# The stores of v, of the output gates and of the merge gates issued by ScalarE in place of SP

## The chip, the core and the metric

The kernel runs on one core of one Trainium2 chip. A core has five engines that take their instructions each in its own order: TensorE (PE), VectorE (DVE), ScalarE (ACT), GpSimd (POOL) and SyncE (SP), and 16 DMA engines that move data between on-chip memory and device memory. A transfer is begun ("issued") by one of the engines' queues; in the kernel before, all of them are issued by SP. The metric is the device time of one execution in microseconds (us), lower is better.

## What is computed

One layer of an encoder with 2048 tokens of width 1024, in fp32. Three token mixers run on one normalised input; their projections are merged by gates, and a squared-ReLU MLP follows. Cut to what matters here:

```python
h = rmsnorm(x, g_mix)
z = h @ w_in
qk_m, v_m, o_m, i_pre, f_pre, qkv_na, q_mem, gate_pre = jnp.split(z, split_idx, axis=-1)
...
h_m = rmsnorm(h_fwd + h_bwd, g_mlstm.reshape(MLSTM_HEADS, MLSTM_V_DIM))
h_m = (h_m.reshape(bsz, s, MLSTM_V_W) * jax.nn.sigmoid(o_m.astype(jnp.float32))).astype(x.dtype)
...
gates = jax.nn.sigmoid(gate_pre).reshape(bsz, s, N_BRANCH, D_MODEL)
y = (gates[:, :, 0] * (h_m @ w_proj_mlstm)
     + gates[:, :, 1] * (h_na @ w_proj_na)
     + gates[:, :, 2] * (h_mem @ w_proj_mem))
x = x + y @ w_out

u = rmsnorm(x, g_ffn) @ w_up
return x + jnp.square(jax.nn.relu(u)) @ w_down
```

`h_fwd` and `h_bwd` are the two directions of an mLSTM over chunks of tokens, which uses `v_m`; `h_na` is attention over a neighbourhood of the token grid with a table of biases, `h_mem` attention to 256 memory tokens.

## The kernel before

**Arithmetic.** A product of fp32 matrices is made of three passes (`mm3`, L233 to L235): each operand is split into a rounded part and a remainder, by ScalarE (a copy) and VectorE (a subtraction). Weights come in units of 512 KB: `fetch` loads a raw unit `wr` (L173, three buffers), ScalarE and VectorE make the split weights `ws` of it (L177, L178, five buffers), and `take` hands them out some units ahead of their use.

**Phases.** Phase 1 goes over four blocks of 512 tokens (`block_a`): query and key for the neighbourhood attention, the convolved query and key of the mLSTM, their value parts, `v`, in blocks 2 and 3 the 24 merge gates, then the output gates. Beside these matmuls, at each `tick`, run pieces of side work: attention units over the grid (their loads `naq`, `nak`, `nav`, and the bias tables `nab`; matmuls at L1055, L1074, L1088), memory attention, and the preparation of the next block (`prep_x` loads `xt`, L463; VectorE normalises it, L418; L435 and L436 split it into `hT`). Between the merge gates of blocks 2 and 3, `sums_down` makes sums of the weights for the MLP: it loads two `xt` tiles (two buffers, L463), VectorE combines them (L583), and they are stored to `s_t`. Phase 2 is the mLSTM by chunks of 128 tokens in both directions (`ml_chunk`, with its loads `qk`, `v`, `rb`, `wb`; the exponentials of decay `de` at L821), its row work by blocks (`ml_rows`: loads `r_f` and `r_i`, scans on VectorE at L754 and L760, `r_b` at L764 stored to `s_r`, `r_w` at L773 stored to `s_w`), and beside them the merge gates of blocks 1 and 0 (`late_gates`). Phase 3 merges, projects, and runs the MLP; `load_mix` loads the branch outputs (L1283) and `merge` loads the gates again (L1294).

**The tiles in question.** A product of `v`, of an output gate or of a merge gate stands in a PSUM bank of tag `mm` (two banks in phases 1 and 2). ScalarE writes it into a tile `ev` of 128 x 512 floats, 256 KB (two buffers in phases 1 and 2), by a copy (L538) or a tanh (L561, L603), and it is stored to device memory: 16 stores of `v` (`s_v`), 16 of output gates (`s_o`) and 96 of merge gates (`s_g`). All go through the helper `store` (L103), as do many other stores of the kernel.

**Order.** Only PE's order is written by hand. The instructions of the other engines, and the DMAs that an engine issues, are ordered by a scheduler which goes by priorities (`cur_priority`) and by its own estimate of when operands are there. An engine takes its list strictly in order. Each transfer is given one of eight semaphores in turn, whichever engine issues it, and is not issued before the earlier transfer on the same semaphore has landed.

Of the kernel before, what the change touches and what calls it, by code (L numbers as in the profile page):

```python
# [34 lines left out]
NAB = 4  # L35
LATER_3 = 4
STORE = 'sync'
ORDER_0 = (2, 3, 0, 1)
WSP, WRAW, AHEAD = 5, 3, 5
NB = S // TB  # L40
# [42 lines left out]
class Body:  # L83
# [15 lines left out]
    def ev(self):  # L99
        return self.t("ev", [128, 512], self.ev_bufs)  # L100

    def store(self, dst, src):
        getattr(self.nc, STORE).dma_start(dst, src)  # L103

    def ps(self, tag, shape=(128, 512)):
        self.n += 1
# [266 lines left out]
    def phase_1(self):  # L373
# [3 lines left out]
        nc.scalar.activation(p_a.tile([128, 16], F32, name="warm"), self.mhalf, AF.Exp)  # L377
        self.xorder = [(0, t) for t in ORDER_0] + [(b, t) for b in range(1, NB) for t in range(4)]
        self.xhs = []
# [110 lines left out]
    def block_a(self, b):  # L490


        nc, a = self.nc, self.a
        hT = self.hT
        w = self.take(4)
        for i, t in enumerate(ORDER_0 if b == 0 else range(4)):
            if i == 0 or b == 0 and i < 3:
                self.trans_x()
            if b == 0 and i == MEM_R:
                self.mem_rms()  # L500
            p = self.tok_group(hT, w, t)
            z = self.t("zna", [128, 512], 4)
            nc.scalar.activation(z, p, AF.Copy)
            self.qkq.append(self.na_qk(b, t, z.rearrange("p (a b) -> p a b", b=32)))
        if b + 1 < NB:
            rms = self.rms_x(b + 1)
            self.jobs += [lambda: next(rms, None), None] * 10
        if b in SPILL:
            for k in range(8):
                self.jobs += [lambda k=k: self.store(self.scr["hT"][b][:, :, k], hT[:, :, k].bitcast(F32)), None]  # L510
        for c in range(4):
            self.conv(b, c, self.ch_group(self.take(1)[0], hT))
        w = self.take(4)
        zif = self.t("zif", [128, 4, 16], 1)
        for t in range(4):
            p = self.tok_group(hT, w, t, slice(0, 256), 4)
            s = self.ev()[:, 0:256]
            nc.scalar.activation(s, p, AF.Copy)

            for half in range(2):  # L520
                for r in range(2):
                    p0 = r * 64 + half * 24
                    self.store(self.scr["vna"][half, 8 * b + 2 * t + r], s[p0:p0 + 40])
            p = self.tok_group(hT, w, t, slice(256, 528), 4)
            z = self.t("zm", [128, 256], 4)
            nc.vector.tensor_copy(z, p[:, 0:256])
            nc.scalar.activation(zif[:, t], p[:, 256:272], AF.Copy)  # L527
            self.memq.append(self.mem_unit(b, t, z))
        for g in {0: [0], 1: [1, 2], 2: [3, 4], 3: [5, 6, 7]}[b]:
            self.na_ready.append(g)  # L530
        self.jobs += [None, None, lambda: self.if_rows(b, zif)]
        w, sums = self.take(4), None
        for t in range(4):
            if t == PREP_V and b + 1 < NB and b not in GATES_1:
                self.prep_x()
            p = self.tok_group(hT, w, t)
            s = self.ev()
            nc.scalar.activation(s, p, AF.Copy)  # L538
            self.store(self.scr["v"][b][t * 128:(t + 1) * 128], s)
            if b == NB - 1 and t % 2 == 0:  # L540
                sums = sums or self.sums_down(15)
                sums = next(sums, None) and sums
        if b in GATES_1:
            sums, qs = None, list(range(7)) if b + 1 < NB else list(range(7, 15))
            for j in range(24):
                if j == 22 and b + 1 < NB:
                    self.prep_x()
                self.gate(b, j)
                if j < 21 or b + 1 == NB:
                    if j % 3 != 1:  # L550
                        sums = sums or self.sums_down(qs.pop(0))
                        sums = next(sums, None) and sums
        w = self.take(4)
        for t in range(4):
            if t:
                self.trans_x()
            if t < 3:
                self.prep_x()
            p = self.tok_group(hT, w, t)
            s = self.ev()  # L560
            nc.scalar.activation(s, p, AF.Tanh, scale=0.5)  # L561
            self.store(self.scr["og"][b][t * 128:(t + 1) * 128], s)
            if b == NB - 1:
                ts = slice(t * 128, (t + 1) * 128)
                src = self.scr["hT"][GATES_2[0]]
                if t < 3:
                    nc.sync.dma_start(hT[:, :, :, ts].bitcast(F32), src[:, :, :, ts])
                else:
                    for k in range(0, 8, 2):
                        for l in range(2):  # L570
                            nc.sync.dma_start(hT[:, l, k:k + 2, ts].bitcast(F32), src[:, l, k:k + 2, ts])
# [27 lines left out]
    def gate(self, b, j, w=None, hT=None, cuts=(0, TB)):  # L599

        p = self.ch_group(w or self.take(1)[0], hT or self.hT, cuts)
        s = self.ev()
        self.nc.scalar.activation(s, p, AF.Tanh, scale=0.5)  # L603
        self.store(self.scr["gate"][b][j], s)

    def late_gates(self, more):

# [982 lines left out]
```

## Time and profile before

| | |
|---|---|
| Time, median of 3 runs | 2939.38 us (2939.16 to 2945.97) |
| The profiled execution: its time | 2945.09 us |
| Its span | 2943.4 us |
| PE busy | 2895.3 us (98%) |
| DVE busy | 2005.5 us (68%) |
| ACT busy | 1186.6 us (40%) |
| POOL busy | 210.0 us (7%) |
| Moved by DMA | 632.00 MB, 215 GB/s |

The page gives busy times of the engines over the span. A view of waits lists, for each engine, what ended its idle time ("waited for"), and for SP how long its next DMA stood in the queue before it could be issued. A timeline lists instructions with their start, and in brackets the idle time before them. PEclk is the clock that was granted to TensorE as a share of its full 2.4 GHz.

### The profile page before, as it was taken

The numbers are of one execution on the slowest core, as the hardware profiler recorded it, in microseconds if no ns is written. First come the engines' busy times: TensorE is split into PE (matmuls) and PEld (weight loads), VectorE is DVE, ScalarE is ACT, GpSimd is POOL, SyncE is SP. The second block draws the span as 40 slices with busy tenths as digits, with TensorE's granted clock in tenths as the row PEclk, the third lists the DMA queues.
The fourth block names the chain that finished last, engine by engine and source line by source line (L and its number), as shares of the span: only waits on it lengthen the run. The fifth ranks groups of instructions, "written<-read, shape, count | busy, mean of one in ns | idle before, by whom it ended". The sixth has DMA issues, their size and how long they took to land.

```text
span 2943.4 us, 41858 instructions
## 1 busy us (share of the span) xinstructions
PE 2895.3 (98%) x15052; PEld 2370.3 (81%) x15052; DVE 2005.5 (68%) x3471; ACT 1186.6 (40%) x2256; POOL 210.0 (7%) x382
## 2 busy tenths in 40 slices
PE   8999999999989999999999999999999999999999
PEld 7888888778868777778888888888788888888887
DVE  6676865477754545655688888666686988886666
ACT  6465654355543333432243333533312433344332
POOL 4121210021000112310000000000000000000000
PEclk9999999999999999999999999999999999999999
DMA  8786778867899777878444445766864444466654
GB/s 287 215 278 201 243 234 249 266 210 221 264 286 300 260 236 233 259 227 303 140 135 157 158 158 194 250 192 221 290 208 117 147 151 154 156 228 219 191 189 161
DMA packets 344976, 632.00 MB, mean 215 GB/s; under 512 B 29664, under 2 KB 151456, under 8 KB 344768
## 3 DMA queue, kind: packets, MB, share of 16 engines
q1 hardware_dynamic: 344768, 629.32, 66.7%
q8 instruction: 119, 1.95, 0.3%
q14 instruction: 89, 0.73, 0.1%
HBM read 452.58 MB, written 176.62 MB: 214 GB/s over the span
## 4 chain that ended last, share of the span: by engine, by line
PE 53%; DVE 1%; DMA 1%; issue 1%; ACT 0%; SPq 0%; POOL 0%; DVEq 0%; ACTq 0%
PE mm L233 18%; PE mm L234 18%; PE mm L235 18%; PE mm L1353 0%; DMA ev<-in_x_dram 0%; DMA wr<-in_w_units_dram 0%; DVE ev L1509 0%; DVE acc L1502 0%; DMA X<-s_a 0%; DVE ws L178 0%; DVE ev L1364 0%; DVE ev L1365 0%; DVE X L1359 0%; DVE ev L1331 0%; PE pn L872 0%
## 5 line engine op out<-in xcount | busy, mean ns | idle before, releaser
L233 PE MATMUL mm<-X,ws 128*128 128x512 f32 x896 | 348.9, 389 | 0.0
L235 PE MATMUL mm<-X,ws 128*128 128x512 f32 x896 | 348.6, 389 | 0.0
L234 PE MATMUL mm<-X,ws 128*128 128x512 f32 x896 | 348.6, 389 | 0.0
L178 DVE TENSOR_TENSOR ws<-wr,ws 128x1024 fp32r<-128x1024 f32 (+1 forms) x194 | 239.1, 1240 | 132.8 <-ACT ws L177 131.4
L233 PE MATMUL mm<-hT,ws 128*128 128x512 f32 (+1 forms) x712 | 293.8, 413 | 0.7 <-ACT ev L561 0.7
L234 PE MATMUL mm<-hT,ws 128*128 128x512 f32 (+1 forms) x712 | 278.4, 391 | 0.3 <-DMA hT<-s_hT 0.3
L235 PE MATMUL mm<-hT,ws 128*128 128x512 f32 (+1 forms) x712 | 278.6, 391 | 0.0
L233 PE MATMUL mm<-ws,hT 128*128 128x512 f32 (+2 forms) x704 | 259.2, 368 | 3.5 <-ACT zif L527 2.1
L177 ACT ACTIVATE ws<-wr 128x1024 fp32r<-128x1024 f32 (+1 forms) x194 | 204.2, 1057 | 121.7 <-PE mm L235 81.9
L235 PE MATMUL mm<-ws,hT 128*128 128x512 f32 (+2 forms) x704 | 249.1, 354 | 2.0 <-DVE hT L436 2.0
L234 PE MATMUL mm<-ws,hT 128*128 128x512 f32 (+2 forms) x704 | 248.3, 353 | 0.0
L235 PE MATMUL mm<-X 128*128 128x512 f32 x600 | 233.5, 389 | 0.5 <-DVE X L1476 0.5
L233 PE MATMUL mm<-X 128*128 128x512 f32 x600 | 233.5, 389 | 0.1
L234 PE MATMUL mm<-X 128*128 128x512 f32 x600 | 233.4, 389 | 0.0
L203 ACT ACTIVATE ws<-wr 128x512 fp32r<-128x512 f32 x224 | 135.0, 628 | 219.9 <-PE mm L235 139.8
L1475 ACT ACTIVATE X<-X 128x1024 fp32r<-128x1024 f32 x108 | 114.7, 1062 | 207.5 <-DMA X<-s_t 66.4
L233 PEld LDWEIGHTS mm<-X,ws 128*128 128x128 f32 x896 | 168.2, 188 | 35.1
L235 PEld LDWEIGHTS mm<-X,ws 128*128 128x128 f32 x896 | 168.2, 188 | 34.9
L234 PEld LDWEIGHTS mm<-X,ws 128*128 128x128 f32 x896 | 168.2, 188 | 34.6
L1476 DVE TENSOR_TENSOR X<-X 128x1024 fp32r<-128x1024 f32 x108 | 131.6, 1223 | 80.1 <-ACT X L1475 79.5
L1502 DVE TENSOR_TENSOR acc<-acc,mm 128x512 f32<-128x512 f32 x192 | 126.3, 684 | 68.7 <-PE mm L235 68.6
L235 PEld LDWEIGHTS mm<-hT,ws 128*128 128x128 f32 x712 | 134.2, 188 | 29.9
(286 smaller groups left out, 6028.6 us busy)
## 6 DMA issues: line engine op xcount, KB each, us to landing
wr<-in_w_units_dram SPq DMA_DIRECT2D x290, 512.0 KB
s_s<-u SPq DMA_DIRECT2D x32, 1024.0 KB
s_g<-ev SPq DMA_DIRECT2D x96, 256.0 KB
ev<-s_g SPq DMA_DIRECT2D x96, 256.0 KB
s_a<-u SPq DMA_DIRECT2D x96, 256.0 KB
X<-s_s SPq DMA_DIRECT2D x42, 512.0 KB
nab<-in_rpb_dram SPq DMA_DIRECT2D x96, 220.0 KB
X<-s_a SPq DMA_DIRECT2D x33, 512.0 KB
```

Source lines behind the costliest of these rows:

```text
L177: nc.scalar.activation(w[:, 0], raw, AF.Copy)
L178: nc.vector.tensor_tensor(w[:, 1], raw, w[:, 0].bitcast(F32), ALU.subtract)
L203: nc.scalar.activation(hi, src, AF.Copy)
L233: mm(out, lhs[0], rhs[0], start=first, stop=False)
L234: mm(out, lhs[0], rhs[1], start=False, stop=False)
L235: mm(out, lhs[1], rhs[0], start=False, stop=last)
L1475: nc.scalar.activation(hi, src, AF.Copy)
L1476: nc.vector.tensor_tensor(lo, src, hi.bitcast(F32), ALU.subtract)
L1502: nc.vector.tensor_tensor(c, c, p, ALU.add)
```

## The change

`store` takes the queue as an argument, and the three calls that store `v`, the output gates and the merge gates name ScalarE. All other stores and all loads stay with SP.

```diff
 STORE = 'sync'
+OWN = 'scalar'
...
-    def store(self, dst, src):
-        getattr(self.nc, STORE).dma_start(dst, src)
+    def store(self, dst, src, queue=STORE):
+        getattr(self.nc, queue).dma_start(dst, src)
...
             nc.scalar.activation(s, p, AF.Copy)
-            self.store(self.scr["v"][b][t * 128:(t + 1) * 128], s)
+            self.store(self.scr["v"][b][t * 128:(t + 1) * 128], s, OWN)
...
             nc.scalar.activation(s, p, AF.Tanh, scale=0.5)
-            self.store(self.scr["og"][b][t * 128:(t + 1) * 128], s)
+            self.store(self.scr["og"][b][t * 128:(t + 1) * 128], s, OWN)
...
         self.nc.scalar.activation(s, p, AF.Tanh, scale=0.5)
-        self.store(self.scr["gate"][b][j], s)
+        self.store(self.scr["gate"][b][j], s, OWN)
```

A new line 38 moves all later lines down by one (L103 becomes L104). PE's order stays the same. 128 DMAs leave SP's list for ScalarE's, and the scheduler, which plans anew, also moves other instructions of SP, ScalarE, VectorE and GpSimd. Three places of it follow; the numbers at the end of names tell tiles apart.

SP at the end of block 2, before: the last output gates of the block are stored (`s_o`), the loads of bias tables (`nab`) and of the next block's tokens (`xt`) come between raw weights (`wr`).

```order
L463 DMA xt_6794<-in_xT_dram 128x1024
L173 DMA wr_6731<-in_w_units_dram 128x1024
L1046 DMA nab_0_0_2_6820<-in_rpb_dram 128x440
L103 DMA s_o_90<-ev_6853 128x512
L1046 DMA nab_0_0_3_6882<-in_rpb_dram 128x440
L103 DMA s_o_90<-ev_6915 128x512
L1038 DMA nav_0_1_6927<-s_vna 120x3x128
L1039 DMA nav_0_1_6927<-s_vna 80x128
L1046 DMA nab_0_1_0_6937<-in_rpb_dram 128x440
L103 DMA s_o_90<-ev_6990 128x512
L173 DMA wr_6993<-in_w_units_dram 128x1024
L463 DMA xt_6856<-in_xT_dram 128x1024
```

And SP at the same place after the change:

```order
L464 DMA xt_6794<-in_xT_dram 128x1024
L1022 DMA naq_1_7123<-s_qs 32x4x256
L1047 DMA nab_0_0_3_6882<-in_rpb_dram 128x440
L464 DMA xt_6856<-in_xT_dram 128x1024
L1023 DMA nak_1_7124<-s_ks 32x4x704
L1022 DMA naq_1_7123<-s_qs 32x4x256
L1047 DMA nab_0_1_0_6937<-in_rpb_dram 128x440
L174 DMA wr_6731<-in_w_units_dram 128x1024
```

The stores are gone from the list, the load `xt_6856` stands three places behind `xt_6794` instead of eleven, and `wr_6731`, which stood ahead of it, comes behind it.

ScalarE in phase 2, before: between two merge gates (`ev`, L603) stand the exponentials of decay (`de`, L821), the denominators (`sm`) and copies (`sk`) of the chunks.

```order
L603 ACTIVATE ev_11759<-mm_11669 128x512
L821 ACTIVATE de_2114_11883<-rb_2086_11754,r_a_2012_11433 128x128 x2
L892 ACTIVATE sm_11804<-pn_11774 128x2
L821 ACTIVATE de_2114_11883<-rb_2086_11754,r_a_2012_11433 128x128
L892 ACTIVATE sm_11804<-pn_11775 128x2
L821 ACTIVATE de_2114_11883<-rb_2086_11754,r_a_2012_11433 128x128
L841 ACTIVATE sk_2062_11655<-mx_11821 128x2x128
L841 ACTIVATE sk_2062_11655<-mx_11822 128x2x128
L603 ACTIVATE ev_11857<-mm_11767 128x512
```

After the change:

```order
L604 ACTIVATE ev_11759<-mm_11669 128x512
L774 ACTIVATE r_w<-r_w 36x512
L104 DMA s_g_92<-ev_11759 128x512
L822 ACTIVATE de_2114_11883<-rb_2086_11754,r_a_2012_11433 128x128
L893 ACTIVATE sm_11804<-pn_11774 128x2
L893 ACTIVATE sm_11804<-pn_11775 128x2
L822 ACTIVATE de_2114_11883<-rb_2086_11754,r_a_2012_11433 128x128 x3
L842 ACTIVATE sk_2062_11655<-mx_11821 128x2x128
L842 ACTIVATE sk_2062_11655<-mx_11822 128x2x128
L604 ACTIVATE ev_11857<-mm_11767 128x512
L851 ACTIVATE sk_2062_11655<-mx_11837 128x256
L104 DMA s_g_93<-ev_11857 128x512
```

Behind each gate now stands its store, one or two places later, and the exponential of the third row unit (`r_w`), which before stood some 20 rows further on, stands between the first of these gates and its store.

SP at the same time, before: the store of the second of these gates, then the loads of the third row unit (`r_f`, `r_i`), whose result goes to `s_r_146` 15 rows below the end of this piece.

```order
L103 DMA s_g_93<-ev_11857 128x512
L750 DMA r_f<-s_lf 4x512
L750 DMA r_i<-s_ig 4x512
L103 DMA s_hf_102<-h_2119_11903 128x512
L809 DMA v_2128_11942<-s_v_85 128x4x128
L750 DMA r_f<-s_lf 4x512
L750 DMA r_i<-s_ig 4x512
```

After the change these loads stand some rows above the piece that follows, which begins with the `r_f` loads of the fourth row unit:

```order
L751 DMA r_f<-s_lf 4x512 x2
L807 DMA qk_2127_11940<-s_qk 128x4x128
L104 DMA s_r_146<-r_b 4x4x128
L104 DMA s_sk_118<-sk_2040_11557 128x768
L174 DMA wr_12156<-in_w_units_dram 128x1024
L813 DMA rb_2172_12145<-s_r_145 128x512
L104 DMA s_hf_112<-h_2098_11810 128x512
L810 DMA v_2107_11849<-s_v_86 128x4x128
```

The row units have moved up against the chunks: the result `s_r_146` now stands ahead of the stores `s_sk_118` and `s_hf_112` and of the load `v_2107`, which all stood ahead of it before.

## Rows read from the trace of the kernel before

**Rows 1.** Busy time, share and instructions of each engine (the page, part 1).

```profile
PE 2895.3 (98%) x15052; PEld 2370.3 (81%) x15052; DVE 2005.5 (68%) x3471; ACT 1186.6 (40%) x2256; POOL 210.0 (7%) x382
```

**Rows 2.** Phases 1 to 3: us, busy PE, PEld, DVE, ACT, POOL; PEclk, DMA share, GB/s.

```profile
0.00:957.00 957.00, 927.54 (x5867) 766.67 (x5868) 612.58 (x1366) 489.48 (x1021) 138.16 (x260) 0.99 0.80 250
957.00:1349.00 392.00, 385.04 (x2156) 296.25 (x2155) 209.25 (x465) 147.42 (x472) 71.88 (x122) 0.99 0.79 249
1349.00:2944.00 1595.00, 1582.70 (x7033) 1307.42 (x7031) 1183.64 (x1640) 549.70 (x764) 0.00 (x0) 1.00 0.56 185
```

**Rows 3.** Waits of PE, whole span: us in total, times, longest.

```profile
PE mx L1055 <- DMA s_g<-ev: 8.5, 1, 8.5
...
PE mm L235 <- DVE hT L436: 2.0, 1, 2.0
...
PE mm L233 <- ACT ev L561: 0.7, 1, 0.7
PE mm L233 <- ACT ev L603: 0.7, 1, 0.7
...
PE mm L233 <- ACT ev L538: 0.4, 1, 0.4
```

**Rows 4.** SP's issues from 870 us: start, us, count.

```profile
870.73 1.59 SPq L463 DMA_DIRECT2D xt<-in_w_units_dram  x2
...
874.47 0.64 SPq L1022 DMA_DIRECT2D nak<-s_ks  x1
...
879.41 0.34 SPq L103 DMA_DIRECT2D s_g<-ev  x1
```

**Rows 5.** Waits of SP's queue, whole span: us in total, times, longest.

```profile
SPq L103 <- ACT ev L603: 85.7, 37, 4.8
...
SPq L463 <- DMA s_t<-xt: 33.2, 20, 4.2
...
SPq L103 <- ACT ev L538: 29.9, 12, 5.2
...
SPq L103 <- ACT ev L561: 21.6, 11, 3.1
```

**Rows 6.** Groups of ScalarE by form: busy us, mean ns, idle us before.

```profile
L603 ACT ACTIVATE ev<-mm 128x512 f32<-128x512 f32 x96 | 56.8, 591 | 115.3 <-issue 58.1 <-PE mm L235 51.2 <-DMA s_g<-ev 5.3
```

**Rows 7.** SP's issues in phase 2, two merge gates in a row.

```profile
1005.19 0.59 SPq L103 DMA_DIRECT2D s_g<-ev  x1
...
1014.06 0.54 SPq L103 DMA_DIRECT2D s_g<-ev  x1
```

**Rows 8.** SP's issues at the end of block 2.

```profile
605.20 0.33 SPq L173 DMA_DIRECT2D wr<-in_w_units_dram  x1
...
614.01 0.33 SPq L463 DMA_DIRECT2D xt<-in_xT_dram  x1
```

**Rows 9.** VectorE's timeline at 618 us, the wait in brackets.

```profile
618.91 2.98 DVE L418 SCALAR_TENSOR_TENSOR xt<-xt,gmix,gbc 128x128 f32<-128x128 f32 x8 [0.84 <-DMA xt<-in_xT_dram]
```

**Rows 10.** Engines busy in three stretches around 618 us.

```profile
614.00:618.00 4.00, 2.81 (x12) 1.69 (x10) 3.63 (x10) 2.13 (x5) 0.84 (x2) 1.00 0.77 252
618.00:623.90 5.90, 3.59 (x17) 2.76 (x17) 5.06 (x15) 2.52 (x6) 3.56 (x4) 1.00 0.79 286
623.90:627.00 3.10, 2.88 (x9) 2.50 (x10) 1.88 (x7) 1.24 (x3) 0.13 (x1) 0.53 0.84 210
```

**Rows 11.** Engines busy in two stretches around 883 us.

```profile
874.30:883.00 8.70, 0.29 (x2) 0.00 (x0) 2.68 (x4) 0.00 (x0) 0.00 (x0) 0.63 1.01 230
883.00:885.60 2.60, 2.48 (x6) 2.08 (x7) 0.84 (x4) 0.66 (x2) 0.00 (x0) 0.50 1.05 406
```

**Rows 12.** SP's issues at the end of phase 2.

```profile
1341.31 1.63 SPq L1283 DMA_DIRECT2D X<-s_hmem  x2
```

**Rows 13.** SP's issues for the third row unit.

```profile
1060.56 0.46 SPq L750 DMA_DIRECT2D r_f<-s_lf  x1
...
1081.34 0.78 SPq L103 DMA_DIRECT2D s_r<-r_b  x2
```

## The prediction

> **What bounds the kernel now.** I read the page's busy shares first. PE is busy 2895.3 us of the 2943.4 us span, ScalarE only 1186.6 us [rows 1]. PE runs the same matmuls in the same order in both kernels, so the change can only move the 48.1 us in which PE stands, and the time that the clock gate takes. Then I cut the span in three stages [rows 2]. PE idles 29.5 us in phase 1 (957.00 less 927.54), 7.0 us in phase 2 (392.00 less 385.04), 12.3 us in phase 3. Phase 3 issues none of the moved stores. So the reachable idle time is at most 36.5 us.
>
> The waits of PE say what ended its idle time [rows 3]. Waits for `ev` tiles (their eviction, and behind it a free buffer) sum to 0.7 + 0.7 + 0.4 = 1.8 us. The largest wait, 8.5 us, is put down to a gate store, but L1055 does not read that tile. It reads `nak` and `naq`; their last load was issued at 874.47, the store only at 879.41 [rows 4]. The store's semaphore event was merely the last one seen. So the stores are not what PE waits for. What they do hold is SP: it stood for a gate, v or output gate tile 85.7 + 29.9 + 21.6 = 137.2 us [rows 5]. Loads queued behind those stores on SP start late, and that is the only way in which the old place of the stores can reach PE.
>
> **The change part by part.** All 128 stores leave SP. One issue holds SP 0.34 us (the store at 879.41 [rows 4]) to 0.59 us (at 1005.19 in phase 2 [rows 7]), so 128 x 0.34 = 44 us of issuing go at the least, 76 us at the most, with up to 137.2 us of standing. None of this is PE time in itself.
>
> *ScalarE gets 128 issues.* The trace before has no DMA issue on ScalarE; the nearest row is SP's issue of the same store. By it ScalarE carries 44 to 76 us more, at most 1263 us of 2943. An issue sits behind an eviction of 591 ns [rows 6], and the next ScalarE instruction starts that much later, also where PE waits for it; but gate stores follow each other at 8.9 us (1005.19 to 1014.06 [rows 7]), and the `mm` tag has two PSUM banks, so an issue is covered: taken as 0. If the cover were gone, all 128 in PE's way would cost 44 to 76 us; nothing in the 1.8 us of waits suggests that. The store now also waits for ScalarE's own write, and for the place of an earlier transfer: see the slower rival.
>
> *The stall at 614 to 627.* SP took the load of raw weights `wr` at 605.20 and the token load `xt` only at 614.01 [rows 8]. VectorE's normalisation of that tile (L418) waited for the load until 618.91 [rows 9], then L436 made `hT`, for which PE waited 2.0 us [rows 3]. Across the three stretches [rows 10] PE idled 4.00 - 2.81, 5.90 - 3.59 and 3.10 - 2.88, in all 3.7 us, and ran the last 3.10 us at a granted 0.53 (near the 1.2 GHz level, after the standing), which loses 1.5 us: 5.2 us together. In the changed order this `xt` load stands ahead of that weight load, with no output gate store before it. I take the whole 5 us off (bounds 0 and 5.2). Late next is the weight load, which moves behind a few loads of 0.3 to 0.4 us each.
>
> *The stall at 874 to 883.* It costs 8.70 - 0.29 us idle, and 2.60 us at a granted 0.50 after it, 1.3 us: 9.7 us [rows 11]. What was late was two `xt` loads at 870.73, waiting for the store of the sums before them (L463 behind `s_t`: 33.2 us in 20 waits [rows 5]); the `nak` loads queue behind [rows 4]. The changed order keeps `xt` ahead of `nak`, and no moved store lies between them. Taken: 0; bounds -9.7 (if sums are made earlier, so that the sums' store lands earlier) and +2.
>
> *Phase 2.* SP's queue interleaves a gate store with the loads of each chunk and the row units. Without the stores these loads come forward by several places. PE idles 7.0 us here at a mean granted clock of 0.99 [rows 2], which is some 4 us more: 11 us can be gained at most, the rest is in rival 2. I take -3, because no wait of PE in this stage is put down to a DMA.
>
> *The merge.* The loads that phase 3 starts on go out up to 1341.31 [rows 12], beside the last gate stores. A store issued at once from ScalarE takes a share of the DMA engines just there. Bounds 0 and +6 (near the 8.7 us that the `nak` loads took under a full DMA share of 1.01 [rows 11]); taken +3. The Trainium skill, "DMA: Bandwidth & Descriptors", section "Queues, rings and completion order", says that each DMA engine takes turns between the rows it has work for, and SP and ScalarE have a row each; by that the store would even overtake loads that SP issued first. The page of the profile shows one hardware queue, so no run here shows it.
>
> The sum is -5 + 0 - 3 + 3 = -5 us against the profiled execution of 2945.1 us, so 2940. That execution lies 5.7 us above the median of 2939.4; against the median the forecast is 2934.4, rounded to **2935**.
>
> **The rivals.** *1. Faster: SP really was the brake.* If sums (VectorE) and loads in blocks 2 and 3 all come forward, the 874 stall goes too: -9.7 with -5, and half of phase 2's 11, -5: about -20, 2919. For it: SP stood 137.2 us for these tiles [rows 5]. Against: VectorE, not SP, often sets when a raw buffer is free, and the `s_t` landing stays.
>
> *2. Slower: ScalarE stands in order for a transfer of SP.* Every DMA takes one of eight semaphores in turn, so a store waits until the transfer eight places before it has landed. Before, both were in one queue; now ScalarE stands if SP has not yet got there, and behind it stand the decay exponentials (L821), the copies and the evictions. The place is the row unit of phase 2: before, its load `r_f` went at 1060.56 and the store of its result `s_r` at 1081.34 [rows 13], 20.8 us of VectorE work apart, with weight, `rb` and `v` loads issued between. In the changed order the next row unit's `r_f` loads and this `s_r` store stand early, ahead of such loads, so SP may stand for VectorE, VectorE for the landing of `s_r`, and ScalarE for the weight load behind. It decides from a wait of about one gate's period, 8.9 us [rows 7]: of a wait of some 16 us, 7 would reach PE. Two such row units are left at that point, so 14 us, and about 2 us of lower clock after each, as at 883 [rows 11]: +18. With the -5 at 614 that is +13, 2952. For it: the orders. Against: the row loads come forward with the store, and then `r_b` is ready when SP comes to it.
>
> *3. No effect.* The loads are early enough anyway, and the stall at 614 only changes its releaser: within 3 us of 2939. The Trainium skill, same page, section "Issuing engines are not separate DMA queues", says that starting DMAs from several engines saves only the issuing sequencer's time; by it the change is worth SP's time of issuing, of which PE pays nothing, so 2939. The rows agree as far as PE's 1.8 us of `ev` waits go; they differ in that SP's standing came to at least 1.8 times its issuing (137.2 against 76).
>
> **How the numbers follow.** A difference of 0.3% (8.8 us) is about what a measurement of this kernel can tell from none. Chances: my forecast (some -10 to +5 us) 0.31, rival 3 0.12; both lie within 0.3%, giving 0.43. Rival 1 and mixtures beyond -8.8 us: 0.30. Rival 2: 0.27. The range goes from rival 1's 2919 to a little beyond rival 2's 2952, as its waits could be longer: 2956. Cut off are all stalls gone at once (-27 us) and a ScalarE that stands at many stores. The likeliest case's own range is 2929 to 2944.
>
> **What would show it.** Right: PE idle at 614 to 627 nearly gone and no granted clock of 0.53 there; the stall near 874 to 883 still there; SP's waits for `ev` gone; ScalarE with idle time in front of its next instruction after a store, but no PE wait for `ev` above 3 us. Rival 1 shows as PE idle in phase 1 under 20 us. Rival 2 shows as PE idle in phase 2 well above 7.0 us, with waits for ScalarE's or VectorE's tiles (L821, L841, `ev`) between 1045 and 1130. The forecast is wrong if the total moves by over 9 us, or if the 614 stall stays and something else pays.

## The result, and the profile after

The changed kernel takes 2950.07 us, the kernel before beside it on the same chip 2942.52 us (medians of 20 runs each): a ratio of 1.0024, 95% interval 1.0015 to 1.0033. It is slower by 7.6 us, where the forecast had -5. The time lies inside the range on record, the change has the other sign. The profiled execution took 2956.77 us with a span of 2954.9 us, 11.5 us above the span before. It lies 6.7 us above its kernel's median, the traced execution of the kernel before 2.6 us above that kernel's, so losses read by comparing the two traces are some 4 us too large in sum.

The page after, parts 1, 3 and 6, first. PE, VectorE and ScalarE do the same work as before [rows 1], and a second hardware queue, q10, has taken 33.56 MB, the 128 stores of 256 KB.

```profile
PE 2896.2 (98%) x15052; PEld 2369.9 (80%) x15052; DVE 2009.1 (68%) x3471; ACT 1187.7 (40%) x2256; POOL 207.0 (7%) x382
...
q1 hardware_dynamic: 326336, 595.75, 63.3%
q10 hardware_dynamic: 18432, 33.56, 3.2%
...
s_g<-ev ACTq DMA_DIRECT2D x96, 256.0 KB
```

The same three stages as in [rows 2] (us, then the busy time of PE, PEld, DVE, ACT, POOL, then PEclk, DMA share, GB/s), after:

```profile
0.00:957.00 957.00, 930.52 (x5886) 769.84 (x5887) 612.07 (x1370) 492.70 (x1026) 138.38 (x260) 0.99 0.81 252
957.00:1349.00 392.00, 371.40 (x2098) 283.10 (x2097) 211.13 (x460) 143.43 (x464) 68.57 (x122) 1.00 0.76 235
1349.00:2955.00 1606.00, 1594.25 (x7071) 1316.94 (x7069) 1185.89 (x1641) 551.54 (x767) 0.00 (x0) 1.00 0.56 186
```

PE idles 26.5, 20.6 and 11.8 us in them, before 29.5, 7.0 and 12.3. So phase 1 gained 3.0 us, phase 2 lost 13.6, phase 3 is as it was. The granted clock is the same, near 2.4 GHz in all three.

**Phase 1** went as forecast. Two windows after, around the two stalls of [rows 10] and [rows 11]; then PE's timeline at the second one (the wait in brackets):

```profile
614.00:627.00 13.00, 11.72 (x59) 9.43 (x58) 9.38 (x25) 7.86 (x18) 6.42 (x7) 1.00 0.88 271
874.00:886.00 12.00, 7.07 (x27) 5.80 (x28) 5.05 (x13) 3.58 (x8) 0.13 (x1) 0.72 0.92 262
```

```profile
878.93 0.61 PE L1056 MATMUL mx<-nak,naq 96*128 96x320 f32 x1 [7.71 <-DMA nab<-in_rpb_dram]
```

At 614 to 627 PE's idle time fell from 3.7 to 1.3 us, and the granted clock of 0.53 is gone. The idle time went with the change: over the same matmuls (from 610 to 635 us in the kernel before) PE stands 0.2 to 1.3 us in the four kernels of this document that store from ScalarE in phase 1 in the new order, and 2.6 to 3.8 us in the eleven others. The low clock is less certain: the clock granted from 608 to 632 us is 0.93 in the kernel before and in "phase 2 alone" below, but 1.00 in the swapped kernel below, and both of these leave phase 1 as it was. Nor do the 3.0 us of the whole phase stand clear by themselves, since the ten kernels that leave phase 1 as it was idle 25.8 to 31.2 us there. At 874 PE still stands 7.71 us for loads of the attention unit, now put down to one of them (`nab`) and not to a gate store.

**Phase 2** is where the time went. The waits of PE between 957 and 1349 us (total, times, longest), first of the kernel before, then after:

```profile
PE tr L914 <- DVE hm L917: 2.6, 3, 2.2
...
PE mx L848 <- ACT sk L841: 0.7, 1, 0.7
```

Of the changed kernel, the waits of PE over the whole span, where the lines are one higher; the `hm` and the L849 waits are all in phase 2:

```profile
PE tr L915 <- DVE hm L918: 10.0, 7, 2.6
...
PE mx L849 <- ACT sk L842: 4.3, 2, 3.2
...
PE mm L234 <- DVE hm L918: 2.0, 1, 2.0
```

10.0 - 2.6, 4.3 - 0.7 and 2.0 make 13.0 of the 13.6 us. `hm` is the end of a chunk: PE transposes its four heads into a bank `tr`, ScalarE (L917) and VectorE (L918) split it into the one buffer `hm`, which two transfers store to `s_hm`; then the next chunk's transposes may follow. The view of this tile, 1150 to 1345 us, before and after (first and last start of each operation; then what its engines stood for, and who stood for it):

```profile
L916 ACT ACTIVATE hm<-tr x16: 572/578/600, 1189.5 to 1319.1; 128x512 fp32r<-128x512 f32 x16
...
its engine sat idle before it (us, times) until:
  ACT hm L916: 4.2, 1
  DMA s_hm<-hm: 0.6, 1
```

```profile
L917 ACT ACTIVATE hm<-tr x16: 571/578/601, 1189.0 to 1330.8; 128x512 fp32r<-128x512 f32 x16
...
  DMA s_hm<-hm: 9.1, 4
  ACT hm L917: 5.7, 2
who waited for it (us, times):
  PEld tr L915: 13.5, 9
  PE tr L915: 10.0, 7
```

The first of the sixteen starts at the same time in both (1189.5, 1189.0), the last 11.7 us later. Followed back over this stretch, the chain that ended last does not run over PE after; two transfers, `s_hm` (14.6% of it) and `og` (11.7%), are its largest named parts (start, us, what):

```profile
1213.33 5.05 DMA s_hm<-hm
...
1222.31 2.99 DMA og<-s_o
1225.40 1.03 DVE og L864
...
1234.93 5.82 DMA s_hm<-hm
...
1252.15 4.07 DMA og<-s_o
```

The longest single wait of PE in phase 2 comes earlier, at a row unit. Its `r_b` scans now stand ahead of `pt` (L840) in VectorE's list, and `pt` and `sk`, which read a chunk's scores, free the PSUM banks of PE's next transposes (L849). VectorE and then PE, after:

```profile
991.46 1.26 DVE L755 TENSOR_TENSOR_SCAN r_b<-reset,r_f 4x512 f32<-4x512 f32 x1 [9.96 <-DMA r_f<-s_lf]
992.65 0.72 DVE L840 TENSOR_TENSOR pt<-mx,de 128x256 f32<-128x256 f32 x2
```

```profile
993.51 0.44 PE L849 MATMUL mx<-ident,qk 128*128 128x128 f32 x2 [3.18 <-ACT sk L842]
```

VectorE stood 9.96 us for the unit's load and PE 3.18 us behind it. In the kernel before the same `pt` runs at 992.52, the scans of this unit only from 999.77, and PE has no such wait.

So PE waits for tiles of VectorE and ScalarE, and these wait for stores and loads of the chunks and of the row units. The prediction had looked only at the first half of that sentence. Two causes can lie behind it: SP's list and VectorE's list are *ordered* differently without the stores (by the two traces some 100 rows of SP and 75 of VectorE from 957 us on have another place), or the large stores now stand in a *second queue* beside SP's loads and other stores. A third is the issue itself, on ScalarE.

### The profile page after: what moved, and what is told of

Its sections match the earlier page's. It is cut to its first block, busy times and chain, and to the rows that moved or that the text cites. A ratio compares the mean times of both kernels' runs of the same rounds, so it can differ in the third digit from the quotient of the medians.

```text
span 2954.9 us, 41863 instructions
## 1 busy us (share of the span) xinstructions
PE 2896.2 (98%) x15052; PEld 2369.9 (80%) x15052; DVE 2009.1 (68%) x3471; ACT 1187.7 (40%) x2256; POOL 207.0 (7%) x382
## 3 DMA queue, kind: packets, MB, share of 16 engines
q10 hardware_dynamic: 18432, 33.56, 3.2%
## 4 chain that ended last, share of the span: by engine, by line
PE 82%; DMA 7%; DVE 5%; issue 2%; ACT 1%; POOL 1%; SPq 0%; POOLq 0%; DVEq 0%; ACTq 0%
PE mm L234 25%; PE mm L236 25%; PE mm L235 25%; PE tr L1075 2%; DMA wr<-in_w_units_dram 1%; DMA s_hm<-hm 1%; DMA s_t<-xt 1%; PE mx L1089 1%; PE mx L1056 1%; DMA qk<-s_qk 1%; DVE ws L179 1%; PE pn L873 1%; DMA xt<-in_w_units_dram 1%; POOL rs L328 1%; PE mx L1226 1%
```

## The experiments

Ratios are to the kernel before on the same chip, with their 95% intervals; the text says "idle" for PE's idle time in the stage 957 to 1349 (392.00 less busy PE), 7.0 us before and 20.6 us after. Diffs are against the changed kernel unless said otherwise.

**Phase 1 alone, phase 2 alone.** The 80 stores of phase 1 from ScalarE and the late gates from SP, and the reverse.

```diff
-    def gate(self, b, j, w=None, hT=None, cuts=(0, TB)):
+    def gate(self, b, j, w=None, hT=None, cuts=(0, TB), queue=OWN):
...
-        self.store(self.scr["gate"][b][j], s, OWN)
+        self.store(self.scr["gate"][b][j], s, queue)
...
-            self.gate(GATES_2[i], j, self.gw, self.h2[i], cuts)
+            self.gate(GATES_2[i], j, self.gw, self.h2[i], cuts, STORE)
```

> Only the 80 stores of phase 1 (v, output gates, merge gates of blocks 2 and 3) go by ScalarE; the 48 late gates stay with SP. In the profiles the changed kernel was 4.5 us ahead of the old one at the start of phase 2 and lost 13 us from there to 1331 us. Theory A (the loss is made in phase 2): this kernel keeps the lead, 2 to 6 us below the kernel before (ratio 0.998 to 0.9995), PE idle in phase 2 near 7 us. Rival B (any move of this kind shakes the whole plan, the place of the loss is chance): the phase 2 part is not near 7 us, ratio anywhere within 0.3%.

> Only the 48 late gates of phase 2 go by ScalarE, phase 1 is as before. Theory A: slower by 8 to 14 us (ratio 1.003 to 1.005), PE idle in phase 2 about 20 us, waits of the transposes (L915) for hm near 10 us. Rival B: no such sum; within 3 us of the kernel before.

Measured: phase 1 alone 0.9990 (0.9979 to 1.0001), phase 2 alone 1.0060 (1.0044 to 1.0075). The stage 957 to 1349 of the two:

```profile
957.00:1349.00 392.00, 384.31 (x2157) 295.02 (x2156) 209.86 (x461) 143.24 (x466) 71.50 (x122) 0.99 0.80 249
```

```profile
957.00:1349.00 392.00, 374.46 (x2110) 286.36 (x2109) 210.92 (x464) 147.56 (x470) 70.00 (x122) 0.99 0.76 234
```

Idle 7.7 and 17.5 us. The loss comes with the 48 late gate stores (15.7 us by the medians). Those of phase 1 are worth a little (3.6 us by the medians, an interval that just reaches 1). The two add up to +12.1 us where the change itself has +7.6, a difference that the intervals allow.

**The same large stores in the old order.** The scheduler's order is held by giving SP something to issue where the store was: one 2 KB row of the same tile (a "token", to a scratch tensor that nobody reads). Against the kernel "phase 2 alone":

```diff
+            tok=[d(f"s_tok{j}", [1, 512]) for j in range(24)],
...
+        if b in GATES_2:
+            self.store(self.scr["tok"][j], s[0:1])
```

> As phase 2 only, but SP also stores one row (2 KB) of each late gate's tile to a spare place. With this SP waits for the tile and issues a DMA just where it did before, and the planner gives all engines the order of the kernel before; the 256 KB still go by ScalarE. Theory O (the loss comes from the new order of SP and VectorE): within 3 us of the kernel before, PE idle in phase 2 near 7 us. Theory Q (it comes from the second queue, ScalarE's 0.33 us per issue or its waits for a place): as slow as phase 2 only, +8 to +14 us.

Measured: 1.0019 (1.0006 to 1.0032), idle 11.0 us: between the two. With tokens beside all 128 stores:

> All 128 stores by ScalarE as in the change, with a 2 KB token by SP beside each one, so that nearly the whole old order stays. Theory O: within 4 us of the kernel before, neither the gain at 614 us nor the loss in phase 2. Theory Q: +5 to +12 us.

Measured: 1.0043 (1.0027 to 1.0058). PE's idle time in phase 1 is 33.6 us here (957.00 less 923.44), 4 above before: in the old order the second queue brings no gain in phase 1 (over the matmuls of the first stall PE stands 3.4 us), so the gain there goes with the new order. This loss was not taken apart further.

**ScalarE's issues.** The kernel before with one more ScalarE operation behind each late gate, 0.31 us in the trace, the price of an issue (0.327 us at the median in the changed kernel):

```diff
+        if b in GATES_2:
+            junk = self.p_a.tile([128, 128], F32, name=f"junk{b}_{j}", tag="junk", bufs=1)
+            self.nc.scalar.activation(junk, self.ident, AF.Copy)
```

> The kernel before, with a copy of 128 x 128 floats (about 0.31 us) on ScalarE behind each of the 48 late gates, into a spare tile; stores stay with SP and the order of all engines stays (two rows differ). It measures ScalarE's time for an issue (0.33 us) by itself. If the 4.8 us that the token kernel of phase 2 lost are ScalarE's time: +3 to +6 us (ratio 1.001 to 1.002). If they come from the second queue or the waits for a place: within 2 us.

Measured: 1.0004 (0.9991 to 1.0017). No cost of ScalarE's time shows. The interval still reaches 5 us; the swapped kernel below, with 48 real issues on ScalarE (of 0.20 us, a smaller transfer), leaves room for some 2 us.

**Which half of phase 2.** The token for some of the late gates only, so that the new order begins late (the condition below), or ends early (`<= 20` in place of `> 20`):

```diff
+        if b in GATES_2 and len(self.gq) > 20:
+            self.store(self.scr["tok"][j], s[0:1])
```

> Late gates by ScalarE, with SP's token beside the first 27 of the 48, so that the old order stays up to about 1190 us and the new order comes after. Theory H (the loop of h, hm and og in the second half of phase 2 is what the new order hurts): some +10 us, most of what phase 2 only lost beyond the token kernel; PE's waits for hm near 8 us. Rival F (the row units at the start of phase 2): as the token kernel, +4 to +6 us.

> The other way round: the token beside the last 21 late gates, so that the new order stands up to about 1190 us and the old one after. Theory H: +4 to +7 us. Rival F: +10 us or more, made before 1010 us. If both halves matter alike: each of the two kernels near +10 us.

Measured: new order in the second half 1.0014 (1.0005 to 1.0023), in the first half 1.0034 (1.0021 to 1.0047); idle 13.0 and 15.4 us. The theory that the loop with the single `hm` buffer at the end of the phase carries the loss (H) fell: the new order in the second half alone adds nothing to the token kernel's 1.0019. That the first half costs more is not shown so clearly, as its interval meets those of the other half and of the token kernel. Nor is the time lost only where the order is new: of the 8.4 us of idle time that the kernel with the new order in the first half has above before, 4.8 lie behind 1200 us.

**Two buffers for `hm`.** If PE only waits because the next chunk's `hm` waits for the store of the last, a second buffer for its rounded part should give most back.

```diff
-        hm = self.t("hm", [128, 2, 4, 128], 1, F32R)
-        nc.scalar.activation(hm[:, 0], p, AF.Copy)
-        nc.vector.tensor_tensor(hm[:, 1], p, hm[:, 0].bitcast(F32), ALU.subtract)
+        hm = [self.t("hm%d" % l, [128, 4, 128], 2 - l, F32R) for l in range(2)]
+        nc.scalar.activation(hm[0], p, AF.Copy)
+        nc.vector.tensor_tensor(hm[1], p, hm[0].bitcast(F32), ALU.subtract)
...
```

> The change, with the first half of the tile hm (written by ScalarE at L917) in two buffers instead of one, so that ScalarE no longer waits for the landing of the store of the tile before. If the landing of these stores (mean 4.0 us with the change, 3.2 before) drives the loss: ScalarE's 9.1 us of waits for it gone, PE's idle time in phase 2 from 20.6 to 12 us or less, at least 6 us below the change. If the order of VectorE alone does it: no gain, within 3 us of the change.

Measured: 1.0009 (1.0000 to 1.0018), some 4 us below the changed kernel by the ratios, whose intervals overlap; but idle is 17.8 us and PE's wait for `hm` still 9.5 us in 6 times. ScalarE's waits for the stores are gone, and VectorE, whose half kept its one buffer and which had no such wait in the changed kernel, now has them:

```profile
DVE hm L918 <- DMA s_hm<-hm: 6.5, 2, 4.7
```

So ScalarE's buffer is at most a part of the cause. A second buffer for both halves was not run, so how much the landing of `s_hm` costs stays open.

**Swapped.** The kernel before, in its own order, with the token on ScalarE and the large store on SP. In the two traces VectorE and GpSimd run the same rows in the same order as in the token kernel, SP and ScalarE too but for the 48 that are exchanged. It has a second queue and ScalarE's issues with their standing; only the 256 KB are elsewhere than in the token kernel.

```diff
         self.store(self.scr["gate"][b][j], s)
+        if b in GATES_2:
+            self.store(self.scr["tok"][j], s[0:1], OWN)
```

> The token kernel of phase 2 with the parts exchanged: SP stores the 256 KB of each late gate as before, ScalarE issues the 2 KB token behind its eviction. The old order stays in every engine, ScalarE has its 0.33 us per issue and its waits for a place, only the large transfer is back on SP. If the token kernel's +4.8 us come from ScalarE's waits for a place (7.7 us of standing there): +3 to +6 us again. If they come from the large store in a second queue (it lands among SP's loads at another time): within 2 us of the kernel before.

Measured: 0.9997 (0.9987 to 1.0008), idle 6.0 us. The token kernel's 1.0019 is about 0.2% or 6 us more, with intervals that overlap a little (1.0006 and 1.0008), and what differs is only which queue holds the large store. VectorE's waits for the output gate loads `og` (256 KB each, issued by SP) differ in the same way. 957 to 1349 us, of the swapped kernel and then of the token kernel:

```profile
DVE og L867 <- DMA og<-s_o: 14.5, 14, 2.0
```

```profile
DVE og L867 <- DMA og<-s_o: 20.5, 14, 2.1
```

From issue to landing (worked out from the semaphore updates in the traces) the 16 `og` loads take 3.08 us on average in the swapped kernel and 3.32 in the token kernel, some 4 of these 6 us. Not all loads of SP are later: `qk` 3.86 and 3.97, `v` 4.35 and 4.25, `sk` 4.50 and 4.15 us.

**The first row unit.** The token for the first gates alone, so that the order is the old one until after the first row unit (R is the theory that this unit's early place loses the time):

```diff
+        if b in GATES_2 and len(self.gq) >= 40:
+            self.store(self.scr["tok"][j], s[0:1])
```

> Late gates by ScalarE, SP's token beside the first 8 of the 48 only: the old order stands to about 1000 us, the new one from there. The kernel with the new order up to 1190 us lost about 10 us, 4 us of it by 1000 us. Theory R (the first row unit, brought forward there, holds SP and ScalarE): +5 to +8 us, 4 us or more below phase 2 only, and no wait of 3 us of PE for sk (L852) near 993. Rival: the loss spreads over the chunks after 1000 us: +10 to +16 us as phase 2 only.

Measured: 1.0053 (1.0039 to 1.0066), as much as "phase 2 alone". PE's wait for `sk` near 993 shrank to 1.1 us (at 996.59), as R had said, but waits of 2.0 and 2.2 us for `sk` stand at 1063.49 and 1095.11 instead. So R fell as the account of the loss in sum: with this unit back in its place, the rows behind lose as much.

**A new order without the large stores in the second queue.** The late gates' 48 stores of 256 KB are left out and ScalarE stores only the token; the merge loads the gates of blocks 2 and 3 also where those of 0 and 1 belong, so that phase 3 moves as much. The order of every engine is that of "phase 2 alone". Against it:

```diff
-        self.store(self.scr["gate"][b][j], s, queue)
+        if b in GATES_2:
+            self.store(self.scr["tok"][j], s[0:1], queue)
+        else:
+            self.store(self.scr["gate"][b][j], s, queue)
...
-                    nc.sync.dma_start(g, self.scr["gate"][b][br * 8 + n])
+                    nc.sync.dma_start(g, self.scr["gate"][b % 2 + 2][br * 8 + n])
```

> The order of phase 2 only in every engine, but ScalarE stores just one row (2 KB) of each late gate, and nobody stores the 256 KB: it leaves out the stores of the late gates (the merge then loads the gates of blocks 2 and 3 for blocks 0 and 1 too). It completes a table of two by two with the old and the new order, with and without the large store through ScalarE's queue. If the new order alone makes the loss beyond the token kernel: +8 to +12 us. If the order only loses because the large stores run beside SP's bursts of loads: within 3 us of the kernel before, or below it.

Measured: 1.0023 (1.0011 to 1.0036). The stage, PE's waits in it and VectorE's wait for `og`:

```profile
957.00:1349.00 392.00, 378.33 (x2126) 290.01 (x2125) 210.25 (x461) 146.09 (x467) 68.10 (x122) 0.99 0.70 212
```

```profile
PE tr L919 <- DVE hm L922: 5.9, 4, 1.6
PE mx L853 <- ACT sk L846: 4.0, 2, 2.7
```

```profile
DVE og L868 <- DMA og<-s_o: 16.4, 14, 1.7
```

Idle is 13.7 us although 12.6 MB less is moved (a DMA share of 0.70 against 0.76): the order alone costs. One row of it can be named. In this kernel VectorE goes through the second row unit's scans from 989.31 on without a long wait, `pt` follows at 998.39, and PE stands behind it:

```profile
999.27 0.48 PE L853 MATMUL mx<-ident,qk 128*128 128x128 f32 x2 [2.75 <-ACT sk L846]
```

And VectorE's wait for `og` is back to 16.4 us, near the 16.8 us of the kernel before. With the stores, in "phase 2 alone", it reads:

```profile
DVE og L864 <- DMA og<-s_o: 20.4, 14, 3.2
```

Four kernels now make a table, each against before (us from the medians; the order new or old, the 256 KB from ScalarE or not):

| late gates | no large store in the second queue | large stores in the second queue |
|---|---|---|
| old order | swapped 0.9997, -1.6 us, idle 6.0 | token 1.0019, +4.8 us, idle 11.0 |
| new order | stores left out 1.0023, +7.0 us, idle 13.7 | phase 2 alone 1.0060, +15.7 us, idle 17.5 |

Between the columns lie 6.4 us in the old order and 8.7 in the new, between the rows 8.6 and 10.9 us. Order and queue each cost several us; whether together they cost more than their sum is not settled, with an uncertainty of 3 to 5 us in each kernel. In the lower left kernel nobody stores the 256 KB, so the 8.7 us hold those bytes as well as their queue; the new order with the large stores on SP was not run.

**A version that beats both.** ScalarE stores in phase 1 only, with the two `hm` buffers; and the two buffers alone in the kernel before.

> Phase 1 only by ScalarE, and hm's first half in two buffers. If the two gains add (3.6 us of phase 1, and up to the 2.6 us that the kernel before waits for hm at L914): 4 to 7 us below the kernel before, ratio 0.9975 to 0.9987, which would beat both kernels. If the second buffer only helped where the store landed late: 3 to 4 us below, as phase 1 only.

> The kernel before with hm's first half in two buffers, all stores on SP. If the gain of the kernel with phase 1 by ScalarE and two buffers (ratio 0.9981) is mostly the buffer's: 0.998 to 0.999. If it is phase 1's: 0.9995 to 1.0005.

Measured: 0.9981 (0.9969 to 0.9993) together, 2938.81 us against 2943.17; the buffers alone 0.9994 (0.9983 to 1.0005), which is no difference. The two stages up to 1349 us of the first:

```profile
0.00:957.00 957.00, 934.16 (x5908) 773.51 (x5909) 614.23 (x1372) 493.95 (x1028) 138.11 (x260) 0.99 0.81 253
957.00:1349.00 392.00, 382.64 (x2159) 293.38 (x2158) 207.67 (x461) 142.53 (x466) 70.73 (x122) 1.00 0.80 251
```

Idle 22.8 us in phase 1 (29.5 before) and 9.4 us in phase 2 (7.0 before): the gain shows in phase 1. By the medians the buffers alone (-1.3 us) and phase 1 alone (-3.6) add up to about the -4.4 measured together, and neither is clear of nothing by itself.

## Why the prediction was wrong

**The step that failed is the phase 2 term, -3 "because no wait of PE in this stage is put down to a DMA".** In its place phase 2 lost 13.6 us of PE time in the profiled execution, and its stores alone cost 15.7 us by the medians. PE indeed never waits for a DMA there; it waits for `hm` and `sk`, and VectorE and ScalarE, which make them, do wait for DMAs. VectorE's 16.8 us for `og` alone stood in the waits of the kernel before, had they been asked engine by engine and not for PE only (phase 1 alone has 17.4 us of them and loses nothing, so such a wait marks a place and not a loss). The step also took "loads come forward" as a gain and left the loss to rival 2. The runs show two losses: the new order of SP and VectorE (1.0023 with the large stores away), 2.75 us of it at a row unit that VectorE takes ahead of a chunk, and the large stores in another queue than SP's loads (1.0019 against 0.9997 in the old order).

Point by point:

- *The issues on ScalarE, taken as 0.* Right. An issue takes 0.327 us at the median, 42.4 us in all, a little under the 44 given as the least. A dummy of that size (1.0004) and a real issue of 2 KB (0.9997) show no cost.
- *The stall at 614, -5.* Right in place and mechanism. PE's 1.3 us of idle time are left of 3.7. Of the 5.2 us, the 1.5 for the low clock are there in some executions only: the swapped kernel, with phase 1 unchanged, runs this place at a granted 1.00. Phase 1 alone measures -3.6 us, if not beyond doubt (0.9979 to 1.0001).
- *The stall at 874, 0.* Right: 7.71 us of it are still there, and the store was not its cause, as [rows 4] had said.
- *SP's waits for `ev`.* Gone for the moved tiles but for 0.3 us, as they must be. Summed over SP's issues in 957 to 1335 us (386 and 325 of them), its issuing fell from 193.9 to 154.7 us as well. Neither shows as a gain in phase 2.
- *The merge, +3.* Not to be told from 0: the idle time of phase 3 is 11.8 us after and 12.3 before. In "phase 2 alone" PE stands 1.4 us for the first loads `X` of phase 3, so the term is not empty either.
- *Rival 2, slower.* Its sign was right, and so was its mark: PE's idle time in phase 2 well above 7.0 us, in waits for VectorE's and ScalarE's tiles. Of its mechanism the first half came true, earlier than it said: the row units moved up, ScalarE stood 10.2 us for the exponential `r_w` of the first unit until 971.68 and VectorE 9.96 us for the load of the second until 991.46, and PE lost 0.7 and 3.2 us behind them. Nothing near 16 us stands between 1045 and 1130. The second half, ScalarE standing at its stores, did not come true. Directly before its 128 issues ScalarE was idle 3.2 us in all, 2.1 us of it in phase 2, at most 1.56 us (at 1210.32). From the end of an eviction to its store there are 39.4 us over all 128 and 10.8 in phase 2, but ScalarE's other rows lie in them; the 7.7 us of standing named for the token kernel were read in the same way, and 1.5 of them are idle time before an issue. The longest such stretch of phase 2, 5.3 us, ends with a wait of `hm` for the landing of its own earlier store, with the gate's store behind it, after which PE idled 2.0 us for `hm`:

```profile
1330.85 0.60 ACT L917 ACTIVATE hm<-tr 128x512 fp32r<-128x512 f32 x1 [4.37 <-DMA s_hm<-hm]
1330.87 0.33 ACTq L104 DMA_DIRECT2D s_g<-ev  x1
```

- *Rival 3.* The Trainium skill, "DMA: Bandwidth & Descriptors", section "Issuing engines are not separate DMA queues", says that a second issuing engine saves only the sequencer's time. By that the token kernel and the swapped one, which have the same order and the same transfers, would take about the same time. They differ by 0.2%, and the profile counts q1 and q10 apart. The measurement decides, for this kernel: what the second engine holds was not neutral.
- *Turns between rows.* The Trainium skill, same page, section "Queues, rings and completion order", has each DMA engine take turns between the rows it has work for. The waits for `og` would fit: in 957 to 1349 us they are 14.5 to 18.7 us in the seven kernels where ScalarE issues no large store in phase 2, and 17.1 to 24.5 in the eight where it does, one of these eight below 19. That this turn-taking is the mechanism is not shown; no run here sees the DMA engines' inner order, and not all of SP's loads landed later.
- *A sum.* The "-27 us" of all stalls gone at once: 5.2, 9.7 and 11 add up to 25.9 us. Nothing hangs on it.

**What stays open** is which of the moved rows costs most. One place is found, the scans of a row unit ahead of `pt`, worth some 3 us of PE; but with the old order kept over it the loss in sum stays, and a second buffer for half of `hm` takes only a part. To settle it the rows would have to be moved back one at a time.

## What to carry to other kernels

Ask for the waits of the engines that feed the bottleneck, not of the bottleneck alone: that PE waits for no DMA says little if VectorE, for whose tile it waits, does. Where a scheduler sets the order, moving a DMA to another engine is two changes, a new order and a new queue; a tiny transfer left in the old place holds the order and lets each be priced. Move a store only in the stage where a row shows the old queue holding up the bottleneck: here phase 1, and not phase 2.

## What was not expected of the hardware

With large stores in a second queue VectorE waited longer for loads of the same size in the first, at the same order and the same bytes: its 14 waits for `og` rose from 14.5 to 20.5 us. And 39 us less issuing on SP in phase 2 bought nothing that shows. SP, too, waits there for tiles of other engines; the largest group of its waits in 957 to 1349 us of the changed kernel is for a chunk's output `h` from VectorE (24.1 us before):

```profile
SPq L104 <- DVE h L899: 21.2, 13, 3.1
```
